# Four products of a Strassen step summed in one PSUM bank, and a gate product moved from GpSimd to VectorE

## The chip, the cores and the metric

The kernel runs on one core of one Trainium2 chip. The metric is the device time of one execution in microseconds (us). The engines of the core work side by side, each through its own instructions in order: TensorE (PE, with its weight loads shown as PEld), VectorE (DVE), ScalarE (ACT), GpSimd (POOL) and SyncE (SP), which issues the DMAs. They wait for each other through semaphores.

## The reference

One encoder layer with the same weights for two batches, 2048 and 1024 positions of 1024 channels (3072 positions in all):

```
z  = rmsnorm(x) @ w_in                      # 1024 -> 512 Fourier + 512 u + 512 v
f  = real(fft2(z_fourier))                  # four groups of 128 channels
u, v = gelu(z_u), gelu(z_v)                 # four heads of 128 channels
sv = w_spatial[h] @ rmsnorm(v)[chunk] + b   # 128 x 128, in chunks of 128 positions
x  = x + rmsnorm(concat(f, u * sv) @ w_out)
a  = rmsnorm(x) @ w_up                      # 1024 -> 2 * 2816
a  = a[s-1] * cw[0] + a[s] * cw[1] + a[s+1] * cw[2] + cb
y  = x + rmsnorm((gelu(a_gate) * a_up) @ w_down)   # 2816 -> 1024
```

All in f32.

## The kernel before

The three large matrix products (into u and v, up, down) are cut into **Strassen steps** (class `Step`, L159 on). One step computes a tile of 256 rows by 1024 columns as 2 x 2 quadrants of 128 x 512. The left operand is a 256-row tile with 1024 contraction rows (quadrants a11 to a22), the right operand stays in SBUF for a whole stage (seven operands `stage.op[j]`). Instead of eight quadrant products there are seven, by Winograd's sums, and one product is 12 matmuls of 512 columns: four blocks of contraction, and three fp32r matmuls each (high x high, high x low, low x high), since each f32 operand is split in a rounded part and its remainder.

What a step does on the engines:

- `load`: two DMAs bring the left tile (`ra0`, `ra1`).
- `sums` (L177 to L180): four GpSimd operations make s1 to s4 (tiles `s0` to `s3`), each from two SBUF tiles.
- `prep(j)` calls `split` (L97 to L100): ACT casts the high part, DVE subtracts it for the low part (tile `wj`). For product 4 of an `Up` step GpSimd subtracts (`POOL = (4,)`).
- `mm(j)`: the 12 matmuls of product j into a PSUM bank of its own (`p0` to `p6`; there are eight banks). The third matmul is the first that reads the low part of `wj`.
- `post(j)` (L201 to L221): ACT copies bank `p0`, and seven DVE additions build the four quadrants c11, c12, c21 and c22 in SBUF, each with one bank as an operand.

The order of the work is written out by hand: `at(slot, order, fn)` puts a function in a slot, one slot per product, and within a slot LOAD comes before PREP, MM, OUT and STORE. The functions run in that order and so set the order on each engine; nothing reorders them. `steps(s, step, ahead=2)` puts the loads six slots ahead, the sums two slots ahead, and product j and its `post` in slot s + j.

Steps have three users:

- `Gate` (12 steps): quadrants (c11, c21) are the two halves of v and (c12, c22) those of u. `vout(j)` applies gelu to one half of v (L414) and takes its sums of squares (L423). `vscale` makes 1/rms on GpSimd (L92, L93), `vnorm` scales v by it in eight DVE operations (L437). `spatial` multiplies on PE (L454 to L456), `gate` multiplies u by the result (L463), `turn` transposes it (L484) and `turned` copies it (L491). Beside these steps GpSimd makes the sums of the output projection's operand (`right_sums`, L125 to L129, tiles `wd` and `wt`).
- `Up` (three blocks of 1024 positions, 22 steps each): a tile of gate channels (c11, c12 to tile `t0`) and one of up channels (c21, c22 to `t1`). `centre` puts each quadrant times the middle tap into t0 or t1 on ACT (L1084); `taps` adds the two neighbours on DVE (L1096), in pieces that depend on the block: 512 or 511 columns in block 0, 256 or 255 in block 2, with single columns at the edges. `gate` (L1132, L1133) takes gelu on ACT and multiplies gate by up on GpSimd. The store writes the tile to `g_d`.
- `Down` (three groups of the contraction, 12 steps each): group 0 has three blocks of contraction instead of four, and 9 matmuls a product. Groups 1 and 2 add the sum of the groups before: `cload` (L1218) fetches it, `cadd` (L1224) adds it on GpSimd (for one row tile of group 2 on DVE). The last two steps of group 2 have a `post` of their own.

Between two stages `turnover` (L233) loads, casts and splits the seven right operands of the next stage (28 tiles, tiles `so...`) while the last steps of the old one run, DVE and GpSimd by turns for the low parts (L155).

The lines on which the steps of the change turn:

```
B11, B21, T4, T2, T3, T1, B22 = range(7)      # which right operand product j takes
self.left = [a11, a12, a22, s2, s3, s1, s4]   # which left operand product j takes
at(s + 5, OUT + 0.2, g.vout, 1)
at(s + 6, OUT + 0.2, u.taps, 1, 0)
at(s + 7, OUT + 0.2, u.taps, 1, 1)
at(s + 8, OUT + 0.2, u.taps, 0, 0)
at(s + 9, OUT + 0.6, u.taps, 0, 1)
at(s + 10, OUT + 0.3, u.gate)
```

## Time and profile before

| | us |
|---|---|
| median of three runs | 2841.45 |
| lowest and highest of the three | 2835.36, 2841.74 |
| the profiled execution | 2835.06 |
| its span | 2833.3 |
| mean granted TensorE clock | 0.983 of full speed |

One execution was profiled; rows and durations of the trace come from it. Its span runs from the first instruction to the last, and 1.8 us lie around it. A row of a timeline has the start, the busy time (of all instructions of the row together), the engine, the line of the kernel and output<-inputs with the number of instructions; in brackets stands how long the engine was idle before it and which instruction ended that wait. A PE row with x2 and then one with x10 and an idle time is a product that stopped after its first two matmuls. Tile names lose the step's number, so that `w6u` is w6 of whichever `Up` step runs then.

### The profile page before, as it was taken

What the parts mean: (1) busy time and instruction counts of PE and PEld (TensorE: products, weight loads), DVE (VectorE), ACT (ScalarE), POOL (GpSimd) and SP (SyncE); (2) the same over time, 40 slices, a digit from 0 to 9 for tenths busy, and PEclk for the clock granted to TensorE, in tenths of its full rate; (3) what the DMA queues carried; (4) which work ended last, traced back from release to release, by engine and by line L of the source; (5) the groups of instructions that cost most, each with busy time, mean ns of one, the idle gap of its engine ahead of it and who ended that gap; (6) DMA issues with size and microseconds to landing.
All of it is one profiled execution on the core that took longest, in us unless ns stands there. A gap on an engine that the chain in (4) does not pass through costs nothing. (4 is left out here: it accounts for less than half of the span.)

```text
span 2833.3 us, 34584 instructions
## 1 busy us (share of the span) xinstructions
PE 2679.7 (95%) x11930; PEld 2165.4 (76%) x11930; DVE 2435.1 (86%) x3251; ACT 1213.1 (43%) x2317; POOL 1640.8 (58%) x1043
## 2 busy tenths in 40 slices
...
GB/s 340 164 159 206 192 245 233 222 177 270 301 100 119 112 100 116 146 120 84 90 67 90 81 157 75 82 68 89 67 116 141 130 216 147 162 193 218 208 213 200
DMA packets 279567, 440.35 MB, mean 155 GB/s; under 512 B 22304, under 2 KB 171296, under 8 KB 279392
## 3 DMA queue, kind: packets, MB, share of 16 engines
...
HBM read 302.81 MB, written 135.28 MB: 155 GB/s over the span
## 5 line engine op out<-in xcount | busy, mean ns | idle before, releaser
L1133 POOL TENSOR_TENSOR t0u<-t0u,t1u 128x1024 f32<-128x1024 f32 x66 | 159.9, 2423 | 385.1 <-ACT t0u L1132 385.0
L198 PE MATMUL p3u<-sox,w3u 128*128 128x512 f32 x792 | 208.7, 404 | 24.5 <-DVE w3u L100 22.0
L1132 ACT ACTIVATE t0u<-t0u 128x1024 f32<-128x1024 f32 x66 | 70.1, 1062 | 326.4 <-DVE t0u L1096 323.8
L198 PE MATMUL p6u<-sox,w6u 128*128 128x512 f32 x792 | 198.7, 394 | 10.2 <-DVE w6u L100 10.2
L198 PE MATMUL p2u<-sox,w2u 128*128 128x512 f32 x792 | 197.7, 398 | 10.2 <-ACT w2u L99 5.6
L100 POOL TENSOR_TENSOR w4u<-s2u,w4u 128x512 fp32r<-128x512 f32 x65 | 101.0, 1553 | 178.6 <-ACT w4u L99 178.6
L198 PEld LDWEIGHTS p3u<-sox,w3u 128*128 128x128 f32 x792 | 147.4, 191 | 74.5 <-DVE w3u L100 42.3
L198 PE MATMUL p0u<-sox,w0u 128*128 128x512 f32 x792 | 192.7, 392 | 7.1 <-DVE w0u L100 4.7
L198 PE MATMUL p1u<-sox,w1u 128*128 128x512 f32 x792 | 193.5, 393 | 5.2 <-DVE w1u L100 5.2
L198 PE MATMUL p4u<-sox,w4u 128*128 128x512 f32 x792 | 194.3, 394 | 2.5 <-DVE w4u L100 2.1
L198 PE MATMUL p5u<-sox,w5u 128*128 128x512 f32 x792 | 191.6, 390 | 4.8 <-ACT w5u L99 3.5
L1084 ACT ACTIVATE t1u<-c21u,cbt,cwt 128x512 f32<-128x512 f32 x66 | 53.9, 817 | 309.2 <-DVE c21u L218 300.0
L198 PEld LDWEIGHTS p2u<-sox,w2u 128*128 128x128 f32 x792 | 148.5, 191 | 49.0 <-DVE w2u L100 11.5
L198 PEld LDWEIGHTS p6u<-sox,w6u 128*128 128x128 f32 x792 | 145.3, 188 | 52.8 <-DVE w6u L100 22.8
L198 PEld LDWEIGHTS p0u<-sox,w0u 128*128 128x128 f32 x792 | 149.4, 189 | 40.0 <-DVE w0u L100 6.0
L198 PEld LDWEIGHTS p4u<-sox,w4u 128*128 128x128 f32 x792 | 151.2, 191 | 35.4 <-DVE w4u L100 2.5
L198 PEld LDWEIGHTS p1u<-sox,w1u 128*128 128x128 f32 x792 | 149.2, 189 | 37.9 <-DVE w1u L100 6.9
L198 PEld LDWEIGHTS p5u<-sox,w5u 128*128 128x128 f32 x792 | 148.5, 188 | 37.7 <-ACT w5u L99 4.3
L100 DVE TENSOR_TENSOR w6u<-s3u,w6u 128x512 fp32r<-128x512 f32 x66 | 159.2, 2412 | 21.1 <-ACT w6u L99 20.7
L206 ACT COPY ud<-p0d 128x512 f32<-128x512 f32 x34 | 19.9, 587 | 344.6 <-PE p0d L198 344.6
L1096 DVE SCALAR_TENSOR_TENSOR t1u<-c21u,cwt,t1u 128x511 f32<-128x511 f32 (+4 forms) x220 | 161.8, 759 | 3.1
L1096 DVE SCALAR_TENSOR_TENSOR t1u<-c22u,cwt,t1u 128x511 f32<-128x511 f32 (+4 forms) x220 | 142.0, 671 | 3.1
...
## 6 DMA issues: line engine op xcount, KB each, us to landing
...
```

Of the source, the lines that this page charges most:

```text
L100: (eng or vec).tensor_tensor(l, src, h.bitcast(F32), op=ALU.subtract)
L198: nc.tensor.matmul(ps, lhsT=w[:, a, k], rhs=op[k][:, b], start=k == 0 and a + b == 0, stop=k == n - 1 and a == 1)
L206: nc.scalar.copy(self.u, p[0])
L1084: nc.scalar.activation(t[:, i], p, AF.Identity, bias=cbt[:, ti : ti + 1], scale=cwt[:, ti, 1:2])
L1096: vec.scalar_tensor_tensor(d, a, w, d, op0=ALU.mult, op1=ALU.add)
L1132: nc.scalar.activation(ga, ga, AF.Gelu_apprx_tanh)
L1133: nc.gpsimd.tensor_tensor(ga, ga, self.t[1], op=ALU.mult)
```

## The change

- The products come in another order (B11, B21, T2, T1, T3, B22, T4), with the left operands permuted to match. The last left operand is a22 itself, the last right operand has its sign turned.
- Products 0, 2, 4 and 6 (`CHAIN`) go into one PSUM bank, `p0`. Only product 0 starts it afresh. After products 0, 2 and 4 ACT copies what the bank holds (into c11, c12 and c22), and the next product of the chain waits on PE for that copy. Four DVE additions follow instead of seven (c11 += p1, c12 += p3, c22 += p3, c12 += p5). Quadrant c21 is what the bank holds after product 6; it is not copied, and those who use it read PSUM.
- `sums` runs one slot earlier (`ahead=3`).
- `Gate`: the second half of v is the quadrant that is ready last, so `vout(1)` comes after product 6, in slot s + 6 instead of s + 5.
- `Up`: gate by up is multiplied on DVE, and the order of the four `taps` is another one.
- `Down`, groups 1 and 2: all products are added by DVE straight into the loaded tiles (eight additions, no copy on ACT and no `cadd`); the loads come at s - 2 instead of s + 3 (or s).

```diff
-    B11, B21, T4, T2, T3, T1, B22 = range(7)
+    B11, B21, T2, T1, T3, B22, T4 = range(7)
+    CHAIN = (0, 2, 4, 6)
...
-            nc.gpsimd.tensor_tensor(b21, b11, b21, op=ALU.subtract)
+            nc.gpsimd.tensor_tensor(b21, b21, b11, op=ALU.subtract)
...
-            self.left = [a11, a12, a22, s2, s3, s1, s4]
+            self.left = [a11, a12, s2, s1, s3, s4, a22]
...
         def mm(self, j):
-            ps = self.p[j] = bank(f"p{j}{self.nm}")
+            chained = j in CHAIN[1:]
+            ps = self.p[j] = self.p[0] if chained else bank(f"p{j}{self.nm}")
...
-                        ps, lhsT=w[:, a, k], rhs=op[k][:, b], start=k == 0 and a + b == 0, stop=k == n - 1 and a == 1
+                        ps, lhsT=w[:, a, k], rhs=op[k][:, b], start=k == 0 and a + b == 0 and not chained,
...
         def post(self, j):
             p, nm = self.p, self.nm
             if j == 0:
-                self.u = half(f"u{nm}")
-                nc.scalar.copy(self.u, p[0])
+                self.c11 = half(f"c11{nm}")
+                nc.scalar.copy(self.c11, p[0])
             elif j == 1:
-                self.c11 = half(f"c11{nm}")
-                vec.tensor_add(self.c11, self.u, p[1])
+                vec.tensor_add(self.c11, self.c11, p[1])
+            elif j == 2:
+                self.c12 = half(f"c12{nm}")
+                nc.scalar.copy(self.c12, p[2])
             elif j == 3:
-                vec.tensor_add(self.u, self.u, p[3])
+                vec.tensor_add(self.c12, self.c12, p[3])
             elif j == 4:
-                self.c21 = half(f"c21{nm}")
-                vec.tensor_add(self.c21, self.u, p[4])
+                self.c22 = half(f"c22{nm}")
+                nc.scalar.copy(self.c22, p[4])
+                vec.tensor_add(self.c22, self.c22, p[3])
             elif j == 5:
-                self.c22 = half(f"c22{nm}")
-                vec.tensor_add(self.c22, self.c21, p[5])
-                vec.tensor_sub(self.c21, self.c21, p[2])
-                vec.tensor_add(self.u, self.u, p[5])
+                vec.tensor_add(self.c12, self.c12, p[5])
             elif j == 6:
-                vec.tensor_add(self.u, self.u, p[6])
-                self.c12 = self.u
+                self.c21 = p[6]
...
-    def steps(s, step, ahead=2):
+    def steps(s, step, ahead=3):
...
-            self.gelu(self.v2, j)
+            self.gelu(self.v2, j, self.p[6] if j else None)
...
-        at(s + 5, OUT + 0.2, g.vout, 1)
+        at(s + 6, OUT + 0.1, g.vout, 1)
...
-            nc.gpsimd.tensor_tensor(ga, ga, self.t[1], op=ALU.mult)
+            vec.tensor_tensor(ga, ga, self.t[1], op=ALU.mult)
...
+            at(s + 5, OUT + 0.1, u.centre, 0)
             at(s + 6, OUT + 0.1, u.centre, 1)
-            at(s + 6, OUT + 0.1, u.centre, 0)
-            at(s + 6, OUT + 0.2, u.taps, 1, 0)
+            at(s + 6, OUT + 0.2, u.taps, 0, 0)
             at(s + 7, OUT + 0.2, u.taps, 1, 1)
-            at(s + 8, OUT + 0.2, u.taps, 0, 0)
-            at(s + 9, OUT + 0.6, u.taps, 0, 1)
+            at(s + 8, OUT + 0.2, u.taps, 1, 0)
+            at(s + 8, OUT + 0.6, u.taps, 0, 1)
...
+            for c in ((c11,), (c11,), (c12,), (c12,), (c22,), (c12,), (c21,))[j]:
+                add(c, c, p[j])
+            if j == 4:
+                add(c22, c22, p[3])
...
-            at(s if d.closing else s + 3, LOAD, d.cload)
-            if not d.closing:
-                at(s + 6, OUT + 0.2, d.cadd, 1)
-                at(s + 7, OUT + 0.2, d.cadd, 0)
+            at(s - 2, LOAD, d.cload)
```

`Gate.post` is changed as `Step.post`, with c11 and c21 in the two halves of `v2` and c12 and c22 in those of `u2`. `Down` of group 0 copies the chain's bank into an SBUF c21 on ACT. Line numbers behind the change are some higher: L1096 becomes L1099, and the sums are L180 to L183.

Three places in the order of the engines. First DVE in an `Up` step of block 2, from the split of w3 to the split of w6, before (the names end in block, step and a running number: step 9 runs, and the taps belong to step 8):

```order
L100 TENSOR_TENSOR w3u_9_16173<-s1u_9_16090,w3u_9_16173 128x512
L209 TENSOR_TENSOR c11u_9_16189<-uu_9_16162,p1u_9_16176 128x512
L1096 SCALAR_TENSOR_TENSOR t0u_8_16138<-uu_8_15997,cwt,t0u_8_16138 128x256 x2
L1096 SCALAR_TENSOR_TENSOR t0u_8_16138<-uu_8_15997,cwt,t0u_8_16138 128x255 x2
L1096 SCALAR_TENSOR_TENSOR t0u_8_16138<-uu_8_15997,cwt,t0u_8_16138 128x1
L1096 SCALAR_TENSOR_TENSOR t0u_8_16138<-c11u_8_16024,cwt,t0u_8_16138 128x256 x2
L1096 SCALAR_TENSOR_TENSOR t0u_8_16138<-c11u_8_16024,cwt,t0u_8_16138 128x255 x2
L1096 SCALAR_TENSOR_TENSOR t0u_8_16138<-c11u_8_16024,cwt,t0u_8_16138 128x1
L100 TENSOR_TENSOR w5u_9_16217<-s0u_9_16089,w5u_9_16217 128x512
L211 TENSOR_TENSOR uu_9_16162<-uu_9_16162,p3u_9_16220 128x512
L100 TENSOR_TENSOR w6u_9_16236<-s3u_9_16092,w6u_9_16236 128x512
```

DVE over the same stretch of the changed kernel (`c12 += p3` is now L218):

```order
L100 TENSOR_TENSOR w3u_9_15848<-s0u_9_15751,w3u_9_15848 128x512
L213 TENSOR_TENSOR c11u_9_15837<-c11u_9_15837,p1u_9_15851 128x512
L1099 SCALAR_TENSOR_TENSOR t1u_8_15813<-c22u_8_15774,cwt,t1u_8_15813 128x256 x2
L1099 SCALAR_TENSOR_TENSOR t1u_8_15813<-c22u_8_15774,cwt,t1u_8_15813 128x255 x2
L1099 SCALAR_TENSOR_TENSOR t1u_8_15813<-c22u_8_15774,cwt,t1u_8_15813 128x1
L1099 SCALAR_TENSOR_TENSOR t0u_8_15794<-c11u_8_15677,cwt,t0u_8_15794 128x256 x2
L1099 SCALAR_TENSOR_TENSOR t0u_8_15794<-c11u_8_15677,cwt,t0u_8_15794 128x255 x2
L1099 SCALAR_TENSOR_TENSOR t0u_8_15794<-c11u_8_15677,cwt,t0u_8_15794 128x1
L100 TENSOR_TENSOR w5u_9_15892<-s3u_9_15754,w5u_9_15892 128x512
L218 TENSOR_TENSOR c12u_9_15890<-c12u_9_15890,p3u_9_15895 128x512
L1136 TENSOR_TENSOR t0u_8_15794<-t0u_8_15794,t1u_8_15813 128x1024
L100 TENSOR_TENSOR w6u_9_15919<-ra1u_9_15685,w6u_9_15919 128x512
```

The taps from c12 (`uu`) have gone forward to the slot before. Behind `c11 += p1` stand those from c22 and from c11; the gate product (L1136) stands ahead of the split of w6, whose source is now the loaded tile instead of the sum s3.

Second GpSimd over the same `Up` steps, from one product 4 to the next, before:

```order
L100 TENSOR_TENSOR w4u_9_16196<-s2u_9_16091,w4u_9_16196 128x512
L1133 TENSOR_TENSOR t0u_8_16138<-t0u_8_16138,t1u_8_16135 128x1024
L177 TENSOR_TENSOR s0u_10_16254<-ra1u_10_16170 128x512
L178 TENSOR_TENSOR s1u_10_16255<-s0u_10_16254,ra0u_10_16169 128x512
L179 TENSOR_TENSOR s2u_10_16256<-ra0u_10_16169,ra1u_10_16170 128x512
L180 TENSOR_TENSOR s3u_10_16257<-ra0u_10_16169,s1u_10_16255 128x512
L100 TENSOR_TENSOR w4u_10_16361<-s2u_10_16256,w4u_10_16361 128x512
```

GpSimd over the same stretch now (the sums are L180 to L183):

```order
L100 TENSOR_TENSOR w4u_9_15875<-s2u_9_15753,w4u_9_15875 128x512
L180 TENSOR_TENSOR s0u_10_15911<-ra1u_10_15845 128x512
L181 TENSOR_TENSOR s1u_10_15912<-s0u_10_15911,ra0u_10_15844 128x512
L182 TENSOR_TENSOR s2u_10_15913<-ra0u_10_15844,ra1u_10_15845 128x512
L183 TENSOR_TENSOR s3u_10_15914<-ra0u_10_15844,s1u_10_15912 128x512
L100 TENSOR_TENSOR w4u_10_16035<-s2u_10_15913,w4u_10_16035 128x512
```

The gate product is gone, and the four sums of the next step follow directly on the split of w4.

Third ACT at the end of a `Gate` step, from the squares of x (`xc`) on, before (`v2g` is the gelu of the second half of v, and `sqg` its squares; `w0g` to `w2g` are casts of the next step):

```order
L314 ACTIVATE xc_1923,ss_6_1986<-xc_1923 128x1024
L99 CAST w0g_1997<-ra0g_1862 128x512
L414 ACTIVATE v2g_1900<-v2g_1900,rall 128x512
L423 ACTIVATE sqg_2017,vsg_1903<-v2g_1900 128x128 x4
L99 CAST w1g_2025<-ra0g_1862 128x512
L414 ACTIVATE u2g_1901<-u2g_1901,rall 128x512
L99 CAST w2g_2061<-ra1g_1863 128x512
```

ACT at the same place now:

```order
L318 ACTIVATE xc_1897,ss_6_1968<-xc_1897 128x1024
L99 CAST w0g_1971<-ra0g_1838 128x512
L99 CAST w1g_1991<-ra0g_1838 128x512
L417 ACTIVATE v2g_1826<-p0g_1813,rall 128x512
L426 ACTIVATE sqg_2021,vsg_1877<-v2g_1826 128x128 x4
L417 ACTIVATE u2g_1827<-u2g_1827,rall 128x512
L99 CAST w2g_2031<-s1g_1944 128x512
```

The gelu of the second half reads the chain's bank (`p0g`), and stands behind two casts for the next step instead of one. Its squares moved with it.

## Rows read from the trace of the kernel before

**Rows 1.** Busy time by engine: us (share of the span) and instructions
```profile
PE 2679.7 (95%) x11930; PEld 2165.4 (76%) x11930; DVE 2435.1 (86%) x3251; ACT 1213.1 (43%) x2317; POOL 1640.8 (58%) x1043
```

**Rows 2.** Stages by window: us, busy by engine (instructions), TensorE clock, DMA share, GB/s
```profile
144.58:352.60 208.02, 199.03 (x971) 165.46 (x970) 173.57 (x261) 106.95 (x287) 128.95 (x103) 1.00 0.55 185
854.00:1200.50 346.50, 346.50 (x1546) 287.11 (x1545) 325.95 (x404) 171.31 (x344) 206.82 (x130) 1.00 0.34 114
1200.50:1256.70 56.20, 43.09 (x169) 31.33 (x168) 54.31 (x55) 31.03 (x61) 39.98 (x25) 0.97 0.44 155
1276.20:1647.90 371.70, 368.71 (x1598) 296.51 (x1598) 360.06 (x552) 156.01 (x247) 198.21 (x115) 1.00 0.24 84
1647.90:1709.20 61.30, 47.27 (x170) 35.38 (x169) 60.81 (x73) 31.05 (x55) 43.42 (x27) 0.86 0.42 153
1751.00:2119.00 368.00, 355.58 (x1514) 279.62 (x1513) 353.34 (x595) 147.81 (x234) 185.00 (x109) 1.00 0.23 80
2381.40:2571.80 190.40, 190.40 (x841) 157.66 (x840) 129.67 (x143) 51.62 (x98) 126.80 (x84) 1.00 0.60 197
2676.60:2796.60 120.00, 118.10 (x505) 93.28 (x504) 115.79 (x109) 40.18 (x72) 97.69 (x62) 1.00 0.68 219
```

**Rows 3.** Timeline of an `Up` step of block 2
```profile
1909.17 2.39 POOL L1133 TENSOR_TENSOR t0u<-t0u,t1u 128x1024 f32<-128x1024 f32 x1 [7.68 <-ACT t0u L1132]
1909.63 2.48 DVE L100 TENSOR_TENSOR w6u<-s3u,w6u 128x512 fp32r<-128x512 f32 x1 [0.49 <-ACT w6u L99]
...
1914.60 2.89 PE L198 MATMUL p0u<-sox,w0u 128*128 128x512 f32 x12
...
1914.92 1.30 POOL L179 TENSOR_TENSOR s2u<-ra0u,ra1u 128x512 f32<-128x512 f32 x1
...
1918.63 0.58 ACT L206 COPY uu<-p0u 128x512 f32<-128x512 f32 x1
...
1920.30 2.97 DVE L1096 SCALAR_TENSOR_TENSOR t1u<-c21u,cwt,t1u 128x256 f32<-128x256 f32 x5
1920.33 1.61 POOL L100 TENSOR_TENSOR w4u<-s2u,w4u 128x512 fp32r<-128x512 f32 x1 [2.40 <-ACT w4u L99]
...
1923.92 2.60 PE L198 MATMUL p3u<-sox,w3u 128*128 128x512 f32 x10 [0.47 <-DVE w3u L100]
1924.38 2.05 DVE L1096 SCALAR_TENSOR_TENSOR t0u<-uu,cwt,t0u 128x256 f32<-128x256 f32 x5
...
1928.91 0.68 DVE L211 TENSOR_TENSOR uu<-uu,p3u 128x512 f32<-128x512 f32 x1
...
1935.04 1.30 PE L198 MATMUL p0u<-sox,w0u 128*128 128x512 f32 x5
```

**Rows 4.** Timeline of a `Gate` step, columns as in rows 3
```profile
213.74 2.91 PE L198 MATMUL p0g<-sog,w0g 128*128 128x512 f32 x12
...
215.24 1.29 POOL L125 TENSOR_TENSOR wt<-wd,wd 128x512 f32<-128x512 f32 x1
...
221.21 5.63 DVE L437 SCALAR_TENSOR_TENSOR v2g<-v2g,rvg_y,gsg 128x128 f32<-128x128 f32 x8
...
221.64 1.34 POOL L177 TENSOR_TENSOR s0g<-ra1g 128x512 f32<-128x512 f32 x1
...
227.50 2.60 PE L198 MATMUL p4g<-sog,w4g 128*128 128x512 f32 x10 [1.32 <-DVE w4g L100]
227.59 1.62 POOL L180 TENSOR_TENSOR s3g<-ra0g,s1g 128x512 f32<-128x512 f32 x1 [1.94 <-DVE w4g L100]
...
234.30 0.72 ACT L414 ACTIVATE v2g<-v2g,rall 128x512 f32<-128x512 f32 x1 [3.20 <-DVE v2g L408]
...
235.38 0.28 PE L454 MATMUL svg<-vhg,wsp 128*128 128x256 f32 x1
...
236.42 0.20 POOL L92 TENSOR_SCALAR rvg_v<-vsg 128x8 f32<-128x8 f32 x1 [4.37 <-ACT sqg L423]
...
236.81 0.86 PE L198 MATMUL p0g<-sog,w0g 128*128 128x512 f32 x3
```

More of the change, by code (lines that the diff above doesn't have):

```diff
@@ L198, in mm @@
                     nc.tensor.matmul(
-                        ps, lhsT=w[:, a, k], rhs=op[k][:, b], start=k == 0 and a + b == 0, stop=k == n - 1 and a == 1
+                        ps, lhsT=w[:, a, k], rhs=op[k][:, b], start=k == 0 and a + b == 0 and not chained,
+                        stop=k == n - 1 and a == 1, skip_group_check=j in CHAIN,
                     )
@@ L393, in post, with gelu @@
         def post(self, j):
[L394 removed]
+            p = self.p
             if j == 0:
[L396 to L398 removed]
                 self.v2 = unit(f"v2{self.nm}", F32, (128, 2, 512))
                 self.u2 = unit(f"u2{self.nm}", F32, (128, 2, 512))
[L401 removed]
+                nc.scalar.copy(self.v2[:, 0], p[0])
+            elif j == 1:
+                vec.tensor_add(self.v2[:, 0], self.v2[:, 0], p[1])
+            elif j == 2:
+                nc.scalar.copy(self.u2[:, 0], p[2])
             elif j == 3:
[L403 removed]
+                vec.tensor_add(self.u2[:, 0], self.u2[:, 0], p[3])
             elif j == 4:
[L405 removed]
+                nc.scalar.copy(self.u2[:, 1], p[4])
+                vec.tensor_add(self.u2[:, 1], self.u2[:, 1], p[3])
             elif j == 5:
[L407 to L414 removed]
+                vec.tensor_add(self.u2[:, 0], self.u2[:, 0], p[5])
+        def gelu(self, t, j, src=None):
+            src = t[:, j] if src is None else src
+            nc.scalar.activation(t[:, j], src, AF.Gelu_apprx_tanh, scale=stats[self.pr].r.col(j))
         def vout(self, j):
@@ L566, in tile_trunk @@
     at(8, PREP + 0.5, heads.sums, 1)
-    for j, s in ((T4, 9), (T2, 10), (T3, 11), (T1, 12), (B22, 13)):
+    for j, s in ((T2, 9), (T1, 10), (T3, 11), (B22, 12), (T4, 13)):
         at(s, PREP + 0.6, heads.prep, j)
```

61 lines of the change are left out of this document (14 added, 47 removed).

## The prediction

> **What bounds the kernel now.** First the busy shares [rows 1]: PE 95% of the span, DVE 86%, GpSimd 58%. PE's matmuls are the same number before and after, so the change can give back at most what PE idles, and the next view is where that is. The windows by stage [rows 2] are to be read as a period per step: an `Up` step has 84 matmuls.
>
> - `Down` group 1: 190.40 us for 841 matmuls, 10.0 steps, PE busy throughout: 19.04 us a step. This is the floor, a product being 2.72 us.
> - `Up` block 0: 346.50 us for 18 steps, PE busy throughout. Block 1: 371.70 for 19 steps, 19.56 each, 0.52 above the floor. Block 2: 368.00 for 18 steps, 20.44 each, 1.40 above.
> - The two turnovers shown: 56.20 us for two steps and 61.30 for two, so 17.6 and 21.3 above the steps around them. There DVE is busy 54.31 of 56.20 and 60.81 of 61.30.
> - `Gate`: 208.02 us for nine steps, 23.1 each. A good part of the 4.1 over the floor is extra PE work (spatial, transposes), the rest waits.
> - `Down` group 2: 120.00 us for six steps, 20.0 each.
>
> Then the timeline of a block 2 step [rows 3] shows why it isn't at the floor. The split of w6 took 2.48 us on DVE where an addition with a PSUM input took 0.68: it started 0.46 after the GpSimd gate product and ended 0.55 after that one. The five taps from c21 took 2.97 beside GpSimd's split of w4, those from c12 2.05 with GpSimd quiet. So a DVE operation on two SBUF tiles and a GpSimd operation take turns, each waiting for the other's whole instruction, and w3, queued behind the taps, reached PE late: product 3 stopped after two matmuls for 0.47 us.
>
> The Trainium skill (SBUF — State Buffer, section "Who interferes with whom") says the same: a DVE instruction with two SBUF inputs contends with a GpSimd instruction that reads SBUF, and the one that comes second blocks fully. The 2.48 against 0.68 agrees.
>
> **The change part by part.** Durations are from the one profiled execution, 2835.06 us.
>
> *Work taken and given.* Per `Up` step DVE loses three of seven additions, at about 0.6 to 0.68 each [rows 3], 1.9 us, and gets the gate product. The trace has no such operation on DVE; twice a 512-column operation is 1.36, less one start, estimated 1.2 to 1.3. GpSimd loses the 2.39 of the gate product. Both are gains of lock time; what they are worth depends on what stands beside the critical splits, so each stage is scheduled anew.
>
> *`Up` block 2.* With t from product 0's start: the bank is copied by ACT at 2.9 (0.58), the casts of w3 and w4 follow to 4.4. GpSimd's split of w4 runs 4.4 to 5.7 (1.30 as the sum s2 [rows 3]). DVE's split of w3 waits for it and ends at 6.25, c11 += p1 at 6.85. Now the order rows of DVE and GpSimd count: the four sums stand directly behind the split of w4, and the taps from c22 behind c11 += p1, so each of the four 256 or 255 wide taps waits behind one sum: four turns of 1.25 + 0.30 from 6.25 on give 12.4. The taps from c11 run free, 2.05, to 14.5, and the split of w5 ends at 15.1. Product 5's third matmul is due at 5 x 2.72 + 0.45 = 14.05. PE stops 1.05, the period is 20.09 instead of 20.44, and 18 such steps give -0.35 x 18 = -6.3. The gate product on DVE comes at 15.6 to 16.9 and the split of w6 ends at 17.6, when its third matmul is due at 16.77 + 1.05 = 17.8: hidden, by 0.2. Bounds: -1.40 x 18 = -25 (the floor) and 0.
>
> *`Up` blocks 1 and 0.* The taps are in fewer pieces: DVE runs 552 instructions in 19 steps and 404 in 18, against 595 in 18 [rows 2]. In block 1 two fewer turns of about 0.3 put w5 at 14.6, 0.6 late: 19.64 against 19.56, +0.1 x 19 = +2 (bounds -0.52 x 19 = -10, and +6). In block 0 w5 is in time or 0.1 late, +2, and I add 2 us for each of four steps at its start in which GpSimd has further sums between: +9 (bounds 0, since PE can't be quicker than busy throughout, and +20).
>
> *`Gate`.* Here the second half of v is now the chain's last quadrant. Its gelu began at 234.30, while product 6 still ran; now it waits for its end, 235.38 [rows 4], and begins at 235.6, 1.3 later. Behind it, in order: the squares, GpSimd's two operations of the root (rvg, from 236.42 on, now 237.7), the wd and wt sums (215.24 to 221.64, 6.4 us), and then the sums for the next step. The sum s0 so starts 9.2 after product 0 instead of 221.64 - 213.74 = 7.9. `vnorm` cannot come forward, since it stands behind the copy of the transposes, 7.5 after product 0, and its eight SBUF operations took 5.63 us by taking turns with GpSimd. Now they meet the end of the wd sums and all four sums: s3 no longer waits for the split of w4 as it did at 227.59 (1.94 idle), because its buffer is free earlier. Four sums of 1.33 end at 14.5, the three vnorm operations left at 15.1 or 15.2, the split of w4 at 15.8. It was needed at 227.50 - 213.74 = 13.76. So PE stops 2.0 us longer in each of some ten full steps: +20. Bounds: 0.8 (the shift of 1.3, less 0.5 for one or two vnorm operations that find a gap) and 2.6 (the shift and one whole sum), +9 to +29. The DVE additions removed lie in slots 5 and 6, where DVE isn't late, and give nothing.
>
> *Turnovers.* DVE and GpSimd share 56 to 61 us of time in which DVE is never free. Per step GpSimd loses 2.4, DVE gains the 1.2 of the gate product, and the taps from c21 read PSUM and so leave the lock, about 1.5: -2.7 a step, five steps over the three turnovers around `Up`: -13.5 (bounds -25, which is what waits for the lock besides, and 0, if ACT's copies, queued behind the casts of the new operands, hold PE's chain).
>
> *`Down`.* Groups 0 and 1 are at the floor: 0. Group 2 loses its GpSimd additions and its DVE additions read a bank each: 19.04 instead of 20.0 for the six steps shown, -6 (bounds -8 and 0: the loads now wait for the stores two steps before, with some 4 us to spare by my count).
>
> *The chained bank.* Products 2, 4 and 6 wait on PE for a copy of 0.58 [rows 3], with one whole product, 2.72, in between. I cost it at nothing; what hides it is that product. What is queued behind the waiting matmul is all of PE. If ACT is held up by another of its operations, it can come late; bounds 0 and 0.5 us x 66 = +33.
>
> Sum: +20 + 9 + 2 - 6.3 - 13.5 - 6 = +5, so 2840 for the profiled execution. The median of the runs stands 6.4 above it (2841.45 against 2835.06), so **2846 us**, +0.2%. What a measurement of this kernel can tell from no change is about 0.3%, 8.5 us: no change.
>
> **The rivals.**
>
> *B, slower: the second half of v behind product 6.* One mechanism, at one place: gelu, squares, root, GpSimd's queue, sums, vnorm, split of w4, product 4. For it: GpSimd is in use 129 of 208 us there and vnorm already takes 5.63. Against: rows 4 show GpSimd idle 1.94 before s3, so some of the shift may be absorbed. At 2.6 us for 11 steps, +29, with the turnovers giving half, -7: +29 + 9 + 2 - 6 - 7 - 6 = +21, 2862. It decides from 2.3 us a step: the other terms make -15, and +8.5 needs 23 from `Gate`.
>
> *C, faster: the contention goes with the gate product.* For it: the two longest stops of DVE in rows 3 stand beside GpSimd's gate product and its split, and DVE has fewer SBUF pairs. Against: by the order rows the sums move into the gap that the gate product leaves. If they meet the taps less than I have them, blocks 2 and 1 fall to 19.04, -25 and -10, turnovers -15, group 2 -6, block 0 nothing, `Gate` +8: -48, 2793.
>
> *D, slower: PE waits for ACT between chained products.* 0.5 us a step in 66 steps, +33: 2879. Against: the copy needs 0.58 and has 2.72. The Trainium skill (PSUM — Partial Sum Buffer, section "Summary: rules for kernel authors") speaks against such a chain: PSUM that is read while matmuls run should be in a different bank. Here reader and writer are one bank, kept apart only by the wait, and no row of before shows how long such a wait is.
>
> **How the numbers follow.** Forecast 0.35, C 0.33, B 0.26, D 0.06. The forecast's own range is 2833 to 2850. The range to 8 in 10 runs from 2806, which leaves the far part of C out (about 0.12), to 2870, past B, leaving D out. Faster by over 0.3% is C, 0.33; the same is the forecast, 0.35; slower is B and D, 0.32.
>
> **What would show it.** Right: `Gate` steps at 25 us with product 4's stop near 3.3; the gelu of the second half of v after product 6; block 2 near 20.1 with product 5 stopping about 1 us for w5; turnovers some 5 us shorter. Wrong: a period of 19.04 in block 2 (C), `Gate` above 25.5 (B), or PE idle behind an ACT copy at the start of products 2, 4 or 6 (D).

## The result, and the profile after

The changed kernel took 2860.96 us (median of four runs, 2858.61 to 2864.66) against 2839.32 for the kernel before in the same runs: a ratio of 1.0078, 95% interval 1.0064 to 1.0092. It is slower by 0.8%. That lies inside the stated range (2806 to 2870), but outside the forecast's own range (2833 to 2850), and the case of the forecast, no change, did not come true. The number is that of rival B (2862).

The profiled execution took 2864.66, its span 2862.6, so the difference to explain is 29.3 us of span. It is the slowest of its four, and the profiled execution of the kernel before was quicker than the others of that kernel: the medians lie 21.6 us apart, so some 8 of the 29.3 belong to the two executions that were profiled. The difference is read stage by stage from the starts of product 0 in the two timelines:

| stretch | before | after | change | forecast |
|---|---|---|---|---|
| to the first `Gate` step | 90.3 | 89.8 | -0.5 | |
| eleven `Gate` periods | 262.3 | 290.4 | +28.1 | +20 |
| from the last `Gate` step to the first `Up` step | 422.9 | 426.2 | +3.3 | |
| `Up` block 0, 21 periods | 425.0 | 431.7 | +6.7 | +9 |
| turnover, blocks 0 to 1 | 56.2 | 56.9 | +0.7 | -5.4 |
| block 1 | 391.2 | 396.6 | +5.4 | +2 |
| turnover, blocks 1 to 2 | 61.3 | 63.5 | +2.2 | -5.4 |
| block 2 | 409.8 | 403.4 | -6.4 | -6.3 |
| turnover, `Up` to `Down` | 53.1 | 54.2 | +1.1 | -2.7 |
| `Down` groups 0 and 1 | 380.7 | 380.2 | -0.5 | 0 |
| turnover to group 2 | 46.7 | 48.4 | +1.7 | 0 |
| `Down` group 2, ten periods | 197.1 | 190.4 | -6.7 | -6 |
| last step and end | 36.7 | 30.9 | -5.8 | |
| sum | 2833.3 | 2862.6 | +29.3 | +5 |

The busy shares of the changed kernel, as [rows 1]:

```profile
PE 2679.8 (94%) x11930; PEld 2188.2 (76%) x11930; DVE 2267.8 (79%) x3045; ACT 1311.8 (46%) x2485; POOL 1344.4 (47%) x907
```

DVE lost 167 us of busy time and GpSimd 296, and the kernel became slower. So neither engine's total bounds it. The windows of the stages, as [rows 2] (us, busy by engine, clock, DMA share, GB/s):

```profile
148.60:352.60 204.00, 183.72 (x866) 152.04 (x865) 148.14 (x209) 103.83 (x269) 104.26 (x90) 0.97 0.50 169
...
1314.90:1691.60 376.70, 367.52 (x1598) 298.21 (x1596) 346.06 (x513) 175.56 (x286) 143.66 (x95) 1.00 0.24 83
1691.60:1755.10 63.50, 47.16 (x169) 36.38 (x168) 59.16 (x71) 33.39 (x60) 36.67 (x24) 0.81 0.39 146
1795.90:2158.50 362.60, 348.21 (x1513) 282.51 (x1512) 332.42 (x558) 166.24 (x271) 129.84 (x90) 1.00 0.23 81
...
2717.40:2831.70 114.30, 114.30 (x506) 94.64 (x506) 95.92 (x103) 38.73 (x66) 73.87 (x49) 1.00 0.69 221
```

`Gate` now needs 25.5 us a step (204.0 for eight) against 23.1, and its mean clock has gone from 1.00 to 0.97. Block 1 has 19.83 a step, block 2 20.14, and group 2 is at the floor, 19.05, with PE busy throughout.

A `Gate` step after, as [rows 4], and products 4 and 5 of the next one:

```profile
301.48 2.91 PE L202 MATMUL p0g<-sog,w0g 128*128 128x512 f32 x12
...
302.39 0.20 POOL L92 TENSOR_SCALAR rvg_v<-vsg 128x8 f32<-128x8 f32 x1 [4.49 <-ACT sqg L426]
...
309.54 6.75 DVE L440 SCALAR_TENSOR_TENSOR v2g<-v2g,rvg_y,gsg 128x128 f32<-128x128 f32 x8
...
310.06 1.34 POOL L180 TENSOR_TENSOR s0g<-ra1g 128x512 f32<-128x512 f32 x1
...
314.04 1.32 POOL L183 TENSOR_TENSOR s3g<-ra0g,s1g 128x512 f32<-128x512 f32 x1
...
316.95 2.60 PE L202 MATMUL p0g<-sog,w4g 128*128 128x512 f32 x10 [2.14 <-DVE w4g L100]
...
325.03 0.69 ACT L417 ACTIVATE v2g<-p0g,rall 128x512 f32<-128x512 f32 x1 [1.74 <-PE p0g L202]
...
326.26 2.91 PE L202 MATMUL p0g<-sog,w0g 128*128 128x512 f32 x12
...
341.67 3.42 PE L202 MATMUL p0g<-sog,w4g 128*128 128x512 f32 x10 [2.09 <-DVE w4g L100]
...
344.90 3.71 PE L202 MATMUL p5g<-sog,w5g 128*128 128x512 f32 x12
```

The chain of the prediction is all there: the gelu waits for PE's product 6 and begins 1.23 before the next product 0 (2.5 before in [rows 4]); the root begins 0.9 after product 0 (0.4 before it then); s0 starts at +8.6; s3 no longer waits; `vnorm` ends at +14.8, and product 4 stops. How much longer it stops must be read from steps of one kind: the step of [rows 4] has eight transposes on PE and stopped 1.32, the step above has sixteen. A step with eight after, and one with sixteen before:

```profile
214.71 2.57 PE L202 MATMUL p0g<-sog,w4g 128*128 128x512 f32 x10 [2.90 <-DVE w4g L100]
```

```profile
297.12 2.56 PE L198 MATMUL p4g<-sog,w4g 128*128 128x512 f32 x10 [0.59 <-DVE w4g L100]
```

So the stop went from 1.3 to 2.9 in the one kind and from 0.6 to 2.1 in the other, by 1.6 and 1.5 us. The last two rows of the step above show what the prediction did not have: after a stop of 2.09 us, ten matmuls took 3.42 and twelve 3.71 instead of 2.60 and 2.89. The windows of two neighbouring steps, with stops of 2.90 and 2.88:

```profile
199.40:224.00 24.60, 21.70 (x107) 17.96 (x106) 18.45 (x27) 11.63 (x33) 12.47 (x10) 1.00 0.46 153
224.00:250.20 26.20, 23.32 (x106) 19.08 (x105) 18.52 (x27) 13.74 (x36) 13.37 (x12) 0.93 0.47 162
```

In about every other step the granted clock falls after the stop from 2.4 GHz to the lower of its two levels, 1.2 GHz, for a mean of 0.93, and the step takes 1.6 us more. The steps at full clock are 1.6 us longer than before, which is the longer stop. The eleven periods as a whole, before and after:

```profile
90.31:352.56 262.25, 244.96 (x1149) 200.99 (x1148) 212.49 (x303) 132.17 (x352) 169.88 (x132) 0.97 0.54 181
```

```profile
89.80:380.21 290.41, 254.54 (x1149) 208.31 (x1148) 208.92 (x277) 146.86 (x373) 158.31 (x132) 0.94 0.48 163
```

PE idles 35.9 us instead of 17.3, 18.6 more, and is busy 9.6 more with the same number of matmuls: about two thirds of the 28.1 us are the stops, one third the clock.

A block 2 step after, as [rows 3]:

```profile
2021.23 2.03 DVE L1099 SCALAR_TENSOR_TENSOR t1u<-p0u,cwt,t1u 128x256 f32<-128x256 f32 x5
2022.31 1.30 POOL L100 TENSOR_TENSOR w4u<-s2u,w4u 128x512 fp32r<-128x512 f32 x1 [12.83 <-ACT w4u L99]
...
2023.56 1.75 POOL L180 TENSOR_TENSOR s0u<-ra1u 128x512 f32<-128x512 f32 x1
...
2024.67 5.34 DVE L1099 SCALAR_TENSOR_TENSOR t1u<-c22u,cwt,t1u 128x256 f32<-128x256 f32 x5
...
2028.14 1.46 POOL L183 TENSOR_TENSOR s3u<-ra0u,s1u 128x512 f32<-128x512 f32 x1
...
2029.94 2.04 DVE L1099 SCALAR_TENSOR_TENSOR t0u<-c11u,cwt,t0u 128x256 f32<-128x256 f32 x5
...
2031.89 0.68 DVE L100 TENSOR_TENSOR w5u<-s3u,w5u 128x512 fp32r<-128x512 f32 x1
...
2032.63 2.56 PE L202 MATMUL p5u<-sox,w5u 128*128 128x512 f32 x10 [0.79 <-DVE w5u L100]
...
2033.16 1.23 DVE L1136 TENSOR_TENSOR t0u<-t0u,t1u 128x1024 f32<-128x1024 f32 x1
```

The five taps from c21, read from PSUM (`p0u`), take 2.03 us, though GpSimd splits w4 beside their second half. Those from c22 take 5.34 us beside the four sums, and those from c11, with GpSimd quiet, 2.04. The split of w5 is late and product 5 stops.

PE's longest waits in the first two turnovers, each from the view of waits of its stretch (waited for: us in total, times, longest):

```profile
PE p0u L202 <- ACT c12u L216: 7.2, 2, 5.2
```

```profile
PE p5u L202 <- DVE w5u L100: 12.7, 2, 6.7
```

The turnover from block 0 to 1 waits for ACT's copy of the bank, the one from 1 to 2 for the split of w5 behind the taps.

### The profile page after: what moved, and what is told of

Read it like the earlier page. It is cut to its first block, busy times and chain, and to the rows that moved or that the text cites. A ratio compares the mean times of both kernels' runs of the same rounds, so it can differ in the third digit from the quotient of the medians.

```text
span 2862.6 us, 34357 instructions
## 1 busy us (share of the span) xinstructions
PE 2679.8 (94%) x11930; PEld 2188.2 (76%) x11930; DVE 2267.8 (79%) x3045; ACT 1311.8 (46%) x2485; POOL 1344.4 (47%) x907
## 4 chain that ended last, share of the span: by engine, by line
PE 44%; DVE 39%; issue 6%; ACT 5%; POOL 3%; DMA 2%; SPq 0%; DVEq 0%; POOLq 0%; ACTq 0%
PE p0d L202 11%; DVE t1u L1099 11%; DVE t0u L1099 6%; PE p0u L202 5%; PE p0g L202 4%; PE p5d L202 3%; PE p3d L202 3%; PE p1d L202 3%; DVE v2g L440 2%; DVE w3u L100 2%; PE pz L345 2%; PE d L656 2%; PE pq L746 2%; PE p5u L202 2%; DVE sox L158 1%
## 5 line engine op out<-in xcount | busy, mean ns | idle before, releaser
L1099 DVE SCALAR_TENSOR_TENSOR t1u<-c22u,cwt,t1u 128x511 f32<-128x511 f32 (+4 forms) x220 | 232.7, 1081 | 3.1
L202 PE MATMUL p0u<-sox,w4u 128*128 128x512 f32 x792 | 197.3, 398 | 10.5 <-ACT c12u L216 9.3
L202 PE MATMUL p0u<-sox,w2u 128*128 128x512 f32 x792 | 193.6, 394 | 5.7 <-ACT c11u L211 4.0
L202 PE MATMUL p0u<-sox,w6u 128*128 128x512 f32 x792 | 193.8, 393 | 3.6 <-DVE w6u L100 3.6
L202 PEld LDWEIGHTS p0u<-sox,w4u 128*128 128x128 f32 x792 | 151.3, 192 | 46.4 <-ACT c12u L216 11.3
L202 PEld LDWEIGHTS p0u<-sox,w2u 128*128 128x128 f32 x792 | 149.7, 190 | 39.0 <-ACT c11u L211 4.8
L202 PEld LDWEIGHTS p0u<-sox,w6u 128*128 128x128 f32 x792 | 149.9, 190 | 37.9 <-DVE w6u L100 6.5
L180 POOL TENSOR_TENSOR s0d<-ra1d 128x512 f32<-128x512 f32 (+1 forms) x36 | 50.2, 1393 | 163.9 <-DMA ra1d<-g_d 137.5
L1099 DVE SCALAR_TENSOR_TENSOR t0u<-c12u,cwt,t0u 128x511 f32<-128x511 f32 (+4 forms) x220 | 122.0, 580 | 3.1
L1099 DVE SCALAR_TENSOR_TENSOR t0u<-c11u,cwt,t0u 128x511 f32<-128x511 f32 (+4 forms) x220 | 118.8, 565 | 3.1
L180 POOL TENSOR_TENSOR s0u<-ra1u 128x512 f32<-128x512 f32 x66 | 117.2, 1776 | 5.5 <-DMA ra1u<-w_up 5.5
```

Of the source, the lines that this page charges most:

```text
L180: nc.gpsimd.tensor_tensor(s1, a21, a22, op=ALU.add)
L202: nc.tensor.matmul(ps, lhsT=w[:, a, k], rhs=op[k][:, b], start=k == 0 and a + b == 0 and not chained, stop=k == n - 1 and a == 1, skip_gro ...
L1099: vec.scalar_tensor_tensor(d, a, w, d, op0=ALU.mult, op1=ALU.add)
```

## The experiments

All ratios are against the kernel before in the same runs, with their 95% interval. The changed kernel has 1.0078.

**E1, the other half of v.** The column halves are exchanged in `Gate`, so that v is c12 and c22.

```diff
-                nc.sync.dma_start(t, wuv[k : k + 2, :, 1 - b].rearrange("k p n -> p k n"))
+                nc.sync.dma_start(t, wuv[k : k + 2, :, b].rearrange("k p n -> p k n"))
...
-        at(s + 1, OUT + 0.2, g.vout, 0)
-        at(s + 6, OUT + 0.1, g.vout, 1)
+        at(s + 4, OUT + 0.2, g.vout, 1)
+        at(s + 5, OUT + 0.2, g.vout, 0)
```

> The changed kernel, with the column halves of the right operand exchanged in the Gate stage alone, so that the two halves of v are the quadrants c12 and c22, ready after products 5 and 4, and the chain's last quadrant is a half of u. Theory (the second half of v is late because it is the chain's last quadrant): the root on GpSimd begins before the next product 0, vnorm meets the sums less, the stop at product 4 falls from 2.1 to under 1 us, and with it go the stretches at a granted clock of 0.93; Gate steps 22.0 to 23.2 us instead of 24.6 and 26.2, 25 to 35 us less in all, 2826 to 2836. Rival (what makes Gate slower is the sums issued one slot earlier and the chain's waits for ACT, not the half of v): Gate steps stay at 24.6 and 26.2, 2861.

Measured: 2872.46, ratio 1.0119 (1.0099 to 1.0139), `Gate` steps of 24.6 to 29.9. Neither theory had that. The timeline of a step:

```profile
305.04 0.72 ACT L417 ACTIVATE v2g<-v2g,rall 128x512 f32<-128x512 f32 x1 [1.36 <-DVE v2g L413]
...
307.16 0.20 POOL L92 TENSOR_SCALAR rvg_v<-vsg 128x8 f32<-128x8 f32 x1 [2.92 <-ACT sqg L426]
...
313.35 8.57 DVE L440 SCALAR_TENSOR_TENSOR v2g<-v2g,rvg_y,gsg 128x128 f32<-128x128 f32 x8
...
322.57 3.57 PE L202 MATMUL p0g<-sog,w4g 128*128 128x512 f32 x10 [3.96 <-DVE w4g L100]
```

The last addition to c12 stands on DVE behind the split of the next step's w0, and this behind a cast that ACT does after the squares of x. So the exchange made the half of v later, not earlier: its gelu began 0.75 after product 0 (at 304.29). The repair failed, but the stop followed the gelu: from 2.14 to 3.96.

**E2, the late half alone, in the kernel before.**

```diff
+            if j:
+                one = S.tile([128, 1], F32, tag="p6one", name=f"p6one{self.nm}")
+                nc.scalar.copy(one, self.p[6][:, 0:1])
             self.gelu(self.v2, j)
...
-        at(s + 5, OUT + 0.2, g.vout, 1)
+        at(s + 6, OUT + 0.1, g.vout, 1)
```

> The kernel before, with one thing of the change done by itself: in Gate, ACT reads one column of bank p6 before the gelu of the second half of v, which so waits for the end of product 6. No chain, and nothing else moved. Theory (the lateness of that half alone makes the Gate stage slow): steps of 24.3 to 26.3 us instead of 23.1, +15 to +30 us, 2855 to 2870. Rival (it takes the earlier sums and the chain as well): at most +0.3 a step, +3 us, 2842.

Measured: 2849.68, ratio 1.0043 (1.0028 to 1.0058): +12 us by the medians, between the two. The steps went to 24.1 to 24.4 and, with a clock of 0.93, to 25.8 and 26.0, but three early ones, which have no squares of x on ACT, stayed at 23.1 to 23.2.

```profile
292.88 0.20 POOL L92 TENSOR_SCALAR rvg_v<-vsg 128x8 f32<-128x8 f32 x1 [6.40 <-ACT sqg L426]
...
306.33 2.56 PE L198 MATMUL p4g<-sog,w4g 128*128 128x512 f32 x10 [1.79 <-DVE w4g L100]
306.42 1.62 POOL L180 TENSOR_TENSOR s3g<-ra0g,s1g 128x512 f32<-128x512 f32 x1 [1.95 <-DVE w4g L100]
```

Here the root was even later than in the changed kernel (1.7 after product 0 against 0.9), and the stop was smaller: 1.79, against 2.14 there and 0.59 before in steps of this kind. What differs is s3: here it waits for w4 and stays out of `vnorm`'s way, as before. In the three early steps the root was as late, and yet the stop stayed at 1.4:

```profile
207.37 1.68 POOL L179 TENSOR_TENSOR s2g<-ra0g,ra1g 128x512 f32<-128x512 f32 x1 [1.88 <-DVE w4g L100]
```

There s2 waits for w4 as well, and `vnorm` meets only two sums. So a late half costs by the sums that then meet `vnorm`: next to nothing with two (the stop 0.1 longer), 1.1 to 1.2 us with three, and 1.5 to 1.6 with all four, as in the changed kernel. The late half so explains the larger part of a stop, and s3, which no longer waits, the rest. The last is argued from these rows: no run sets s3 free and changes nothing else.

**E3 and E4, the gate product.** E3 is the changed kernel with the product back on GpSimd, E4 the kernel before with it on DVE.

```diff
 E3
-            vec.tensor_tensor(ga, ga, self.t[1], op=ALU.mult)
+            nc.gpsimd.tensor_tensor(ga, ga, self.t[1], op=ALU.mult)
 E4
-            nc.gpsimd.tensor_tensor(ga, ga, self.t[1], op=ALU.mult)
+            vec.tensor_tensor(ga, ga, self.t[1], op=ALU.mult)
```

> The changed kernel with the gate product of Up back on GpSimd, and the chain as it is. Theory (with the gate product gone, GpSimd runs the four sums directly behind the split of w4, beside the taps from c22; with it back the sums come only after the gelu, when those taps are over): the taps from c22 take 2.1 us instead of 5.3 in block 2, product 5 does not stop, blocks 1 and 2 run at 19.04 to 19.4 a step, 25 to 38 us less than the changed kernel, 2823 to 2836, if the turnovers lose nothing. Rival (the gate product on GpSimd is what blocks DVE, as the change has it): block 2 at 20.4 or above and block 1 at 19.6 or above, +5 to +15, 2866 to 2876.

> The kernel before with the gate product of Up on DVE, nothing else. Theory (the place of the sums decides): the sums follow directly on the split of w4 and meet the two tap sets from c12 and c11 behind c11 += p1; w5 comes later than before, block 2 at 20.8 to 22 and block 1 at 19.7 to 20.5 a step, +10 to +40 us, 2850 to 2880. Rival (the gate product on GpSimd is the block): block 2 at 19.0 to 20.0, -10 to -30, 2810 to 2830.

Measured: E3 2846.26, ratio 1.0032 (1.0018 to 1.0045); E4 2902.92, ratio 1.0231 (1.0214 to 1.0247). With the kernel before and the changed one this is a table of two by two for the `Up` stage (us from the first `Up` step to the second step of `Down`, profiled executions):

| | before | chain alone (E3) | gate on DVE alone (E4) | both |
|---|---|---|---|---|
| block 0 | 425.0 | 433.9 | 454.7 | 431.7 |
| turnover | 56.2 | 56.1 | 57.1 | 56.9 |
| block 1 | 391.2 | 383.0 | 414.7 | 396.6 |
| turnover | 61.3 | 56.8 | 63.1 | 63.5 |
| block 2 | 409.8 | 411.4 | 426.8 | 403.4 |
| turnover | 53.1 | 51.0 | 53.3 | 54.2 |
| sum | 1396.6 | 1392.2 | 1469.7 | 1406.3 |

The gate product on DVE costs 73 us alone, and still 14 with the chain. The theory of E3 held for block 1, where PE never idles, but not for the whole (2846 against 2823 to 2836):

```profile
1311.10:1672.80 361.70, 361.70 (x1597) 299.52 (x1596) 321.62 (x495) 179.94 (x287) 191.37 (x116) 1.00 0.25 87
```

E4 came out in its theory's direction and dearer than its range (2903 against 2850 to 2880; block 1 at 20.7 a step against 19.7 to 20.5). There the sums meet the taps from c21 and c12, as the waits in block 2 and one set of taps show:

```profile
PE p3u L198 <- DVE w3u L100: 15.6, 17, 0.9
PE p5u L198 <- DVE w5u L100: 12.3, 17, 0.7
```

```profile
1983.68 5.02 DVE L1096 SCALAR_TENSOR_TENSOR t1u<-c21u,cwt,t1u 128x256 f32<-128x256 f32 x5
```

For block 2 of E3 its theory failed: 20.55 a step.

```profile
1999.19 4.12 DVE L1099 SCALAR_TENSOR_TENSOR t0u<-c12u,cwt,t0u 128x256 f32<-128x256 f32 x5
...
2003.97 2.56 PE L202 MATMUL p0u<-sox,w2u 128*128 128x512 f32 x10 [0.86 <-DVE w2u L100]
...
2006.98 2.05 DVE L1099 SCALAR_TENSOR_TENSOR t1u<-c22u,cwt,t1u 128x256 f32<-128x256 f32 x5
...
2012.22 2.41 POOL L1136 TENSOR_TENSOR t0u<-t0u,t1u 128x1024 f32<-128x1024 f32 x1 [8.92 <-ACT t0u L1135]
```

The taps from c22 are quick as foreseen, but the sums come behind the gate product and run over into the next step, where they hold the taps from c12, and w2 behind them.

**E5, an order of its own for `Gate`.** T4 runs fourth in its own bank; the half of v needs one addition more.

```diff
+        SEQ, LINKS = (0, 1, 2, 6, 4, 3, 5), (2, 4)
...
+            elif j == 4:
+                nc.scalar.copy(self.u2[:, 1], p[4])
+                vec.tensor_add(self.v2[:, 1], self.u2[:, 1], p[6])
...
-        at(s + 6, OUT + 0.1, g.vout, 1)
+        at(s + 5, OUT + 0.2, g.vout, 1)
```

> The changed kernel with an order of its own for the seven products of a Gate step: T4 runs fourth, in a bank of its own, and the second half of v is the copied partial sum plus that bank (one DVE addition more), ready after the fifth product; chain, sums one slot earlier and GpSimd's work stay. Exchanging the column halves made the half of v still later (its gelu 0.75 us after the next product 0, against 1.2 before it in the changed kernel and 2.5 before it in the kernel before), and the stop at product 4 grew to 3.96. Theory (the stop follows the time of that gelu by about one to one): the gelu comes 3 us or more before the next product 0, the stop falls to 0 to 0.6, the granted clock stays at 1.00, Gate steps 22.0 to 23.2, -25 to -32 us against the changed kernel, 2829 to 2836. Rival (the earlier sums and ACT's copies are the cause): steps above 24, 2855 or more.

Measured: 2843.84, ratio 1.0015 (1.0003 to 1.0028), 17 us under the changed kernel. Four of the first steps took 22.2 to 23.6, near the theory; the later ones 24.3 to 26.5, above it. The stop did not follow the gelu one to one: this came 3.6 to 5.3 us before the next product 0, and yet the stop was 0.9 to 1.9 in those first steps and 1.7 to 2.9 in the later ones. A new wait shows, that of the first wt sum for its load:

```profile
289.41 1.29 POOL L128 TENSOR_TENSOR wt<-wd,wd 128x512 f32<-128x512 f32 x1 [2.03 <-DMA wd<-wd]
...
302.11 2.56 PE L203 MATMUL p0g<-sog,w4g 128*128 128x512 f32 x10 [1.86 <-DVE w4g L100]
```

**E6 and E7, the splits ahead of the taps.** In E6 the gate product is on DVE, in E7 on GpSimd.

```diff
-            at(s + 6, OUT + 0.2, u.taps, 0, 0)
-            at(s + 7, OUT + 0.2, u.taps, 1, 1)
+            at(s + 7, PREP + 0.5, u.taps, 0, 0)
+            at(s + 8, PREP + 0.5, u.taps, 1, 1)
             at(s + 8, OUT + 0.2, u.taps, 1, 0)
-            at(s + 8, OUT + 0.6, u.taps, 0, 1)
-            at(s + 10, OUT + 0.3, u.gate)
+            at(s + 10, PREP + 0.5, u.taps, 0, 1)
+            at(s + 11, OUT + 0.3, u.gate)
```

> The changed kernel with the taps of Up moved behind the splits of the same slot: from c12 behind w2, from c21 behind w3, from c11 behind w5, and the gate product (on DVE still) behind w6. Theory (what stops PE is only that the split of w5 stands behind taps that wait for GpSimd's sums): product 5 no longer stops, blocks 1 and 2 at 19.04 to 19.5 a step, -20 to -35 us against the changed kernel, 2826 to 2841. Rival (DVE has too much to do whatever the order): the stop moves to another product and blocks 1 and 2 stay within 0.2 of 19.8 and 20.1, 2855 to 2865.

> As the kernel with the splits first, but with the gate product on GpSimd, where block 1 ran at 19.04 and block 2 at 20.55 because the four sums ran over into the taps from c12 ahead of w2. Theory: with w2 ahead of these taps block 2 too comes to 19.04 to 19.5, block 1 stays at 19.04, -30 to -45 us against the changed kernel, 2816 to 2831. Rival (the taps then hold w3 instead): block 2 at 20.2 or above, 2838 or more.

Measured: 2905.79, ratio 1.0238 (1.0222 to 1.0253), and 2938.77, ratio 1.0347 (1.033 to 1.0364). Both theories missed. E6 is dearer than its rival too (2855 to 2865), and E7 lies far above the bound of its own (2838 or more): block 1 ran at 19.95 and 20.4, block 2 at 20.7 and 21.3, and block 0 left the floor. A row of E6 in block 1 shows why moving taps is dear:

```profile
1455.71 1.21 DVE L1099 SCALAR_TENSOR_TENSOR t0u<-halo,cwt,t0u 128x1 f32<-128x1 f32 x1
...
1457.58 2.58 PE L202 MATMUL p3u<-sox,w3u 128*128 128x512 f32 x10 [0.17 <-DVE w3u L100]
```

A tap of a single column, with two SBUF inputs, took 1.21 us: it stood behind a whole sum. Moved behind w2, the taps from c12 met GpSimd's split of w4 and its first sum, and w3 was late instead.

**E8, the edge copies.** In block 0 ACT's copies of one column (`part`) go from behind the taps to just ahead of the gelu.

```diff
                 add(to[:, 0:511], e[:, 1:512], w2)
-                nc.scalar.copy(part[:, one], to[:, 511:512])
...
             ga = self.t[0]
+            if self.blk == 0:
+                for gu in range(2):
+                    ti = gu * NFT + self.ft
+                    nc.scalar.copy(part[:, ti : ti + 1], self.t[gu][:, 1, 511:512])
```

> The changed kernel with ACT's copies of one edge column in block 0 moved from behind the taps to just ahead of the gelu of the gate. Theory (in the turnover from block 0 to block 1 ACT, in order, waits for the taps at such a copy, the copy of the bank after product 2 stands behind it, and PE waits 7.2 us for that): that wait goes, the two steps from 1238 to 1295 take 4 to 8 us less, 2853 to 2857 in all. Rival (there DVE and GpSimd wait for each other whatever ACT does): 0 to -2, PE waits for a split instead, 2859 to 2861.

Measured: 2865.8, ratio 1.0091 (1.0075 to 1.0106). The wait for the copy of c12 went, and others came:

```profile
PE p5u L202 <- DVE w5u L100: 10.1, 2, 6.7
PE p0u L202 <- DVE w6u L100: 4.3, 1, 4.3
```

The two steps took 60.4 us against 56.9, longer even than the rival had it. This fits the rival's cause: in this turnover the splits on DVE set the pace, and ACT's wait only stood in front of them. Why the two steps became longer is not shown.

**E9 and E11, the squares of x.** E9 is E5 with the line below, E11 the changed kernel with it.

```diff
-            at(s - 3, OUT + 0.5, stats[pr].scale)
+            at(s - 4, OUT + 0.5, stats[pr].scale)
```

> The kernel with Gate's own order of products, and the squares of x (ACT, on the tiles xc) one slot earlier, ahead of ACT's copy of the bank after T3. With the order alone the first five steps ran at 22.2 to 23.6 and the later ones, which have these squares, at 24.2 to 26.5; there the first of the wd and wt sums waited 2.0 us for its load, which SP issued 3.1 us before the next product 0, as in the changed kernel, against 5.3 in the kernel before. Theory (the copy, which waits for the product's end, holds up the squares behind it, these the release of the buffers, and that the loads of the left tile and of wd): the load is issued 5 us or more before the next product 0, all Gate steps come to 22.0 to 23.4, -8 to -15 us against the order alone, 2829 to 2836. Rival (the later steps have more work on PE and ACT, and that is all): no change, 2844.

> The changed kernel with the squares of x one slot earlier and nothing else. Theory (in the changed kernel the late half of v decides, and the sums follow directly on the root, so that an earlier load helps nothing): Gate steps stay at 24.6 and 26.2, 0 to -5 us, 2856 to 2862. Rival (the loads held up by ACT's copies are what makes the changed kernel's Gate steps slow): the later seven steps fall by 1.5 or more, 2845 to 2850.

Measured: E9 2835.18, ratio 0.999 (0.998 to 0.9999); E11 2861.25, ratio 1.0089 (1.0072 to 1.0105). E11 came out as its theory had it, but it is no test of the loads: from the third step on they were issued 3.3 to 3.6 us before the next product 0, against 2.8 to 3.6 in the changed kernel. E9 gave 9 us over E5, and its steps came to 22.5 to 23.9 but for one of 25.3; the mechanism is only half that of the expectation. The gelu came earlier, 4.9 before the next product 0, and the stop fell to 1.06, but the load was issued only 3.6 us before that product (302.76 against 306.34), and the sums still waited for it:

```profile
284.12 1.42 POOL L128 TENSOR_TENSOR wt<-wd,wd 128x512 f32<-128x512 f32 x1 [2.31 <-DMA wd<-wd]
...
297.05 2.58 PE L203 MATMUL p0g<-sog,w4g 128*128 128x512 f32 x10 [1.06 <-DVE w4g L100]
```

In E5 as in E9 the root is over when this wait for the load begins. So the load is what ended last in both, and E9's gain in these steps is the load: the first sum began 1.5 us after product 0 (284.12 against 282.66) instead of 2.5 (289.41 against 286.93).

**E10, put together.** E9, with the gate product on GpSimd in block 1 and on DVE in blocks 0 and 2.

```diff
-            vec.tensor_tensor(ga, ga, self.t[1], op=ALU.mult)
+            (nc.gpsimd if self.blk == 1 else vec).tensor_tensor(ga, ga, self.t[1], op=ALU.mult)
```

> The same, and in block 1 of Up the gate product on GpSimd, in blocks 0 and 2 on DVE, which is what was faster in each. Expected from the periods by block: block 1 at 19.04 a step instead of 19.82, the turnover behind it 5 us shorter, block 2 at 20.12: -15 to -22 us against the kernel above, 2810 to 2820, faster than the kernel before by 0.7 to 1%. Rival (the gain of one stage is lost in the next, as the turnovers did): 2825 or more.

Measured: 2816.36, ratio 0.9929 (0.9917 to 0.9942), faster than both kernels. Block 1, the turnover behind it and block 2:

```profile
1286.50:1648.20 361.70, 361.70 (x1597) 299.62 (x1596) 322.12 (x495) 179.52 (x285) 189.45 (x115) 1.00 0.25 86
1648.20:1705.00 56.80, 42.62 (x169) 32.13 (x168) 54.78 (x66) 31.80 (x57) 42.90 (x25) 0.94 0.43 155
1748.80:2111.00 362.20, 348.12 (x1513) 282.38 (x1512) 332.06 (x558) 166.24 (x271) 129.80 (x90) 1.00 0.24 81
```

Block 1 is at the floor, the turnover 6.7 us shorter than in the changed kernel, and block 2 as in the changed kernel.

## Why the prediction was right in its parts and wrong in its sum

*`Up` block 2* was right, term and mechanism: -6.4 against -6.3, a period of 20.14 against 20.09, product 5 stopping for w5 behind the taps and the sums (0.79 where 1.05 was forecast).

*Blocks 1 and 0* were right in sign (+5.4 and +6.7 against +2 and +9). In block 1 the mechanism was right too, and its size too small: product 5 stopped for w5 in all of 19 steps, 0.5 us each, and the step is 19.83 instead of 19.64. In block 0 the sum is in part luck: four steps run at 20.3, but they are spread over the block instead of standing at its start, and product 6 stops there for w6; the first two steps add 2.0 more, and in the second of them product 4 waits 2.1 us for ACT's copy.

*`Down` group 2* was right: the floor, -6.7 against -6. The last step and the end, -5.8, were not costed: there the kernel before stopped products 0, 1 and 5 for their splits, 3.3 us in all, and the changed one does not.

*`Gate`* had the right mechanism and too small a size: +28.1 against +20. The stop itself came to 1.6 us a step, somewhat under the 2.0 forecast. What was missing is the clock: a stop of 2 to 3 us is followed in about every other step by a stretch at the lower level, 1.6 us each. The eleven periods took 262.3 us before, 273.6 with the late half alone (E2), 290.4 in the changed kernel (287.5 to 291.5 in E3, E6, E7 and E8, which have the same `Gate`), 274.2 with an earlier half (E5) and 266.3 with the load earlier as well (E9). So neither the late half nor the chain with its earlier sums makes the 28.1 alone; in E5 and E9 chain and earlier sums stay, and most of it goes. The chain's waits for ACT are no rival in the steady steps: from the second step on PE has one stop a step, that for w4. The loads did not bind in the changed kernel, where the first wt sum waited at most 0.35 us for its own. That rival B came so near in its sum is luck in part: it had 2.6 us a step and +29 without the clock, and -7 for turnovers that measured +4.0.

*The turnovers* are the step that failed: "-2.7 a step, five steps", -13.5, and measured +4.0 (0.7 + 2.2 + 1.1; E1, E5, E9 and E11, with the same `Up` steps, have +2.0 to +3.9), 17.5 of the 24 us by which the sum was off. The reckoning took GpSimd's and DVE's busy time as one account, from which the 2.4 of the gate product is taken and to which 1.2 is added. By the two by two, the chain alone gives -6.7 there, near the -7.5 (1.5 a step) booked for the taps from c21, and the gate product on DVE takes back 10.7, where another -6 (1.2 a step) had been booked. So the term that failed is the gate product. [rows 2] had shown which engine is the full one: DVE 54.31 of 56.20, GpSimd 39.98. Moving work from the one with slack to the one without cannot be booked as a gain. In what order it stands matters besides: in the turnover from block 1 to 2, w5 behind the taps waited up to 6.7 us.

*The chained bank* was rightly costed at nothing in the steady steps. In the turnover from block 0 to 1 PE did wait for the copies of c12 (7.2 us), but in E8 that wait goes and others take its place.

*Rival C* was wrong for the reason given against it: the sums moved into the gap that the gate product left. E3 shows that the gate product on GpSimd brings block 1 to the floor, but not block 2, where the sums come late (20.55 a step).

The Trainium skill (SBUF — State Buffer, section "Who interferes with whom") says that issue order, not the shape of an operation, decides which engine blocks. The single-column tap of 1.21 us in E6 agrees. It also counts a DVE instruction with at most one SBUF input, outside the two-port modes, as free of the contention with GpSimd. The taps from c21 agree: 2.03 us from PSUM in the changed kernel, with GpSimd's split of w4 beside them, against 5.34 from SBUF beside the sums.

What stays open: why s2 waits for w4 in the three early steps of E2 and not in the later ones, and why of two steps with the same stop one loses clock and the other does not.
